# Which steps of two interleaved attentions wait for each other on TensorE

## The chip, the cores and the metric

One Trainium2 chip, one core. The metric is the device time of one execution in microseconds (us), as the median of a few executions. A kernel's profile is one more execution, with an instruction trace; its times are counted from the start of the span. TensorE is called PE, VectorE DVE, ScalarE ACT, GpSimd POOL, SyncE SP (it issues the loads).

## The reference

Two layers of an encoder on 272 tokens (16 meta tokens and a grid of 4 x 64) of width 2048, all in float32. In short:

```python
for l in range(2):
    gq, gk, gv, gr, glr, nq, nk, nv = split(h @ w_in[l])      # one projection, 6176 columns
    g = log_sigmoid(glr @ w_up + b_up) / 16                   # decay, forward and backward
    o = gla_scan(gq, gk, gv, g_fwd) + flip(gla_scan(flip(...), g_bwd))   # 4 heads, dk 128, dv 256
    y_gla = rms_norm(o) * norm_w * silu(gr)
    y_na = neighbourhood_attention(nq, nk, nv, rel_bias)      # 16 heads of 64, window 4 x 16 and the metas
    h = layer_norm(alpha * h + concat(y_gla, y_na) @ w_out)
    h = layer_norm(alpha * h + square(relu(h @ w_ff1)) @ w_ff2)   # 2048 -> 8192 -> 2048
```

The metas are dropped from the output (256 x 2048).

## The kernel before, in words

**Products.** Activations lie transposed, features on the partitions and tokens (272, or 256 where the metas are no longer needed) along the row. A float32 product is made of three single-pass products of a rounded type (fp32r): each operand is split into a high part (a rounding copy on ACT) and a low part (a subtraction on DVE), and high*high, low*high and high*low are added in PSUM. So every weight block of 128 x 1024 that SP loads is split on the way (`halves`, lines L217 on ACT and L218 on DVE; tiles `raw`, `wh`, `wl`, three buffers each). One output tile of 128 features is made in two halves: `eight` (L252) issues the products of one weight block, which are 24 at 272 columns, or 16 (at 512 and 256 columns in turn) where 256 tokens are enough, and two of them make an output. `by_k` (L293) and `sixteen` (L264) are the same work in other loops. These products are called main products below.

**What runs beside them.** While the projection's main products run, the two attentions are done piece by piece. Both are Python generators: each `yield` ends a step. `by_m` calls `pump(fg, bg, meet)` after every half output, and `pump` takes `fg` steps of the foreground queue and `bg` steps of the background queue; shares of a step are kept as credit. The linear attention's four heads (`gla_head`) are the background. While the gate columns r are projected it gets 1.3 steps a half (`GLA_R`), and while the 24 output tiles of the neighbourhood attention (q, k, v of eight pairs of heads) are projected it gets 1.4 (`GLA_NA`). The foreground has one step a half: the gates of the linear attention (`silu`), then the pairs of the neighbourhood attention (`na_pair`).

**Steps with products of their own.** Products whose operands were not split run as float32 in several passes: an instruction of this kind has two records in the trace.

- In `gla_head`: `group(0)` (L608 and L612, blocks of 32 columns), called G0 here; `group(4)` with L659, L663 and L667, called G4; then, after `am` and `parts` (the scores `A`, split by ACT at L319 and DVE at L320), the product of scores and values, L689 to L693, called o here, which is fp32r; then `mean` (split `sp`, product L934 with a matrix of 1/n), fp32r.
- In `na_pair`: the scores L747 and L751 of one pair, together with the output product L808 and L813 of the pair before (`na_out`), called N here; and the transposes L769 to L776, called T, which have one record each.

**Who waits.** A generator that yields True says that its next step should meet one of the other queue. `pump` holds such a step of the background back until a foreground step of the same kind ran in the same call, but at most `MEET` half outputs:

```python
            if self.bg and self.wants.get(self.bg[0]):
                alone = meet and not some
                if ran or alone and self.late < MEET:
                    self.late += alone and not ran
                    self.credit = min(self.credit, 2)
                    break
```

Even where nothing is met (`meet` is False while r is projected) the test `ran` makes such a step the first background step of its half.

**Order on the engines.** The program's order is not the order on an engine. A scheduler places each instruction by its priority and by when its own model of the chip says that the operands are there; on the chip each engine then runs its list in order, and waits where an operand is not there.

Of the kernel before, what the change touches and what calls it, by code (L numbers as in the profile page):

```python
# [31 lines left out]
EPS = 1e-5  # L32
TAU = 16.0
NEG = -1e30
GLA_R, GLA_NA, NORMS = 1.3, 1.4, (1.0, 0.6)
LEAD = 4
WARM = 14
MEET = 2
PAD = 40
PITCH = 288  # L40
WIDE = 1280
# [17 lines left out]
class Trunk:  # L59
# [66 lines left out]
    def pump(self, fg, bg, meet=False):  # L126
# [10 lines left out]
        while self.credit >= 1:  # L137
# [4 lines that stand above are left out]
# [417 lines left out]
    def gla_head(self, h):  # L559
# [117 lines left out]
        high, low = wide(parts, L), wide(parts[:, 1], L)  # L677
        self.split(wide(A, 3 * P), high, low)
        yield
        yield True  # L680
        while 2 * h + 1 not in self.gate:
            yield True
        os_ = []
        rs, tn = (g2.tile([P, L], F32, name=nm, tag=nm, bufs=1)[:, :n] for nm in ("grs", "gtn"))
        for e in range(2):
# [48 lines left out]
    def na_pair(self, c, q, k, v):  # L734
        nc, b = self.nc, self.a2
        heads = [slice(hh * NAD, hh * NAD + NAD) for hh in range(2)]
        two = lambda a: a.rearrange("p (t c) -> p t c", t=2)
        bias = b.tile([P, 4, NKEY], F32, name="nb", tag="nb")
        nc.sync.dma_start(bias, self.i["nab"][self.l, c])
        s = b.tile([P, 4, NKEY], F32, name="ns", tag="ns")  # L740
        st = b.tile([P, 12], F32, name="nst", tag="nst")
        if self.due:
            self.due()
        ps = self.spare(2)
        for t in range(2):
            for hh, hs in enumerate(heads):
                nc.tensor.matmul(ps[hh][:, t * NKEY:t * NKEY + NKEY], lhsT=q[hs, NM + t * P:NM + t * P + P], rhs=k[hs, t, :],  # L747
                                 start=True, stop=True)
        if self.full:
            for hh, hs in enumerate(heads):  # L750
                nc.tensor.matmul(ps[hh][:, 2 * NKEY:2 * NKEY + NK2], lhsT=q[hs, :P], rhs=k[hs, 0, P:],  # L751
                                 start=True, stop=True)
            meta = self.nms[c % 2]
            sm = meta[:NM, :, :NK2]
        for hh in range(2):
            nc.vector.tensor_tensor(s[:, 2 * hh:2 * hh + 2, :], two(ps[hh][:, :2 * NKEY]), bias[:, 2 * hh:2 * hh + 2, :], ALU.add)
            if self.full:
                nc.vector.tensor_tensor(sm[:, hh, :], ps[hh][:NM, 2 * NKEY:2 * NKEY + NK2], self.qmask, ALU.add)
        pr = self.npr[c % 2]
        self.softmax(s, st, 4, ((s[:, :, :P], s[:, :, :P]), (pr[:, :, :NK2], s[:, :, P:])))  # L760
        yield
        if self.full:
            mt = b.tile([NM, 6], F32, name="mst", tag="mst")
            self.softmax(sm, mt, 2, ((sm, sm),))
        yield
        yield True
        pv, *pts = self.bank(), *self.spare(2)
        for t in range(2):
            nc.tensor.transpose(pv[:, t * P:t * P + P], v[0][:, t, :], self.ident)  # L769
        nc.tensor.transpose(pv[:, T:T + P], v[1].rearrange("p t c -> p (t c)"), self.ident)  # L770
        for hh, pt in enumerate(pts):
            for t in range(2):
                nc.tensor.transpose(pt[:, t * P:t * P + P], s[:, 2 * hh + t, :P], self.ident)  # L773
            nc.tensor.transpose(pt[:, T:T + P], pr[:, 2 * hh:2 * hh + 2, :].rearrange("p u c -> p (u c)"), self.ident)
            if self.full and hh:
                nc.tensor.transpose(pt[:, T + P:], meta.rearrange("p u c -> p (u c)"), self.ident)  # L776
        v1 = b.tile([P, 2, P], F32, name="v1", tag="v1")
        v2 = b.tile([P, P], F32, name="v2", tag="v2")
        nc.scalar.copy(v1, two(pv[:, :T]))
        nc.vector.tensor_copy(v2, pv[:, T:T + P])  # L780
        p1 = b.tile([P, 4, P], F32, name="p1", tag="p1", bufs=1)
        p2 = b.tile([P, 2, P], F32, name="p2", tag="p2", bufs=1)
        for hh, pt in enumerate(pts):
            nc.scalar.copy(p1[:, 2 * hh:2 * hh + 2, :], two(pt[:, :T]))
            nc.vector.tensor_copy(p2[:, hh, :], pt[:, T:T + P])
        pm = None
        if self.full:
            pm = self.npm[c % 2]
            for hh, hs in enumerate(heads):
                nc.vector.tensor_copy(pm[hs, hh, :], pts[1][hs, T + P:T + P + NM])  # L790
        self.due = lambda: self.na_out(c, v1, v2, p1, p2, pm)
        yield True
        if c == 7:
            self.due()
            yield
# [131 lines left out]
    def mean(self, src, n, i=0, pool=None):  # L927

        parts = [t[:, :src.shape[-1]] for t in self.pair(pool or self.lp, "sp", i)]
        self.split(src, *parts)  # L930
        yield True
        p = self.bank()[:, :src.shape[-1]]
        for i, v in enumerate(parts):
            self.nc.tensor.matmul(p, lhsT=self.ones_r[n], rhs=v, start=i == 0, stop=i == 1)  # L934
        return p
# [297 lines left out]
```

## Time and profile before

| what | value |
|---|---|
| median of 3 executions | 2332.03 us (2331.26 to 2332.49) |
| the profiled execution, its span | 2332.43 us, 2330.6 us |
| PE busy | 2319.4 us, 100% of the span |
| DVE, ACT, POOL busy | 65%, 52%, 6% |
| granted PE clock | nine tenths or more in all 40 slices |
| DMA | 419.02 MB, 180 GB/s on average |

The stages that matter here: in layer 0 the columns of the neighbourhood attention are projected from 160 to 342 us, in layer 1 from 1346 to 1520 us, with r just ahead of them. A row of the timeline gives the start, the length, the engine, the source line and what is written and read; matmuls overlap one another, so the start of the next row tells more than the length. Four main products of 272 columns and the two after them are one group of six.

### The profile page before, as it was taken

To read this page: it belongs to the slowest core of one execution; us is meant where nothing else is said; L and a number is where in the kernel's file an instruction comes from. 1 tells how busy PE (TensorE), PEld (TensorE's weight loads), DVE (VectorE), ACT (ScalarE), POOL (GpSimd) and SP (SyncE) were. 2 spreads that over 40 slices of the span, in tenths; PEclk is the share of its full clock that TensorE was granted. 3 is DMA by queue.
4 is the path that set the end of the run, shared out by engine and by line. 5 is a ranking of instruction groups with operands and counts; after the bars stand their busy time and mean duration, and the time that the engine had idled before them with its cause. 6 is when DMAs were issued, how large, how long until landed. Compare 5 with 4: busy or idle time off the path is not lost.

```text
span 2330.6 us, 44637 instructions
## 1 busy us (share of the span) xinstructions
PE 2319.4 (100%) x18180; PEld 2208.1 (95%) x18180; DVE 1519.6 (65%) x2432; ACT 1221.6 (52%) x2100; POOL 129.4 (6%) x200
## 2 busy tenths in 40 slices
PE   9999999999999999999999999999999999999998
PEld 9999999999999999999999899989988888888888
DVE  5588777775544455547576887778866545666655
ACT  5666665564433344444456666655655334555443
POOL 0021110110000000000020111100100000000000
PEclk9999999999999999999999999999999999999999
DMA  8554445555555555555555555445665666666664
GB/s 264 155 163 153 153 142 173 175 178 181 180 181 181 180 180 177 180 181 180 179 180 170 175 161 164 158 155 190 190 196 189 194 197 188 193 197 214 199 194 149
DMA packets 118302, 419.02 MB, mean 180 GB/s; under 512 B 13513, under 2 KB 14025, under 8 KB 118097
## 3 DMA queue, kind: packets, MB, share of 16 engines
q1 hardware_dynamic: 117808, 415.65, 56.7%
q8 instruction: 142, 2.33, 0.4%
q14 instruction: 64, 0.52, 0.1%
q10 hardware_dynamic: 288, 0.52, 0.1%
HBM read 414.03 MB, written 2.10 MB: 179 GB/s over the span
## 4 chain that ended last, share of the span: by engine, by line
PE 97%; DVE 2%; ACT 1%; issue 0%; DMA 0%; SPq 0%; DVEq 0%; ACTq 0%
PE mm L252 57%; PE mm L264 29%; PE mm L293 6%; PE bg L293 1%; PE bg L808 1%; PE mm L747 1%; PE bg L608 1%; DVE wl L218 1%; PE bg L454 0%; ACT wh L217 0%; PE mm L773 0%; DVE acc L1036 0%; DMA raw<-in_win 0%; PE bg L934 0%; PE mm L497 0%
## 5 line engine op out<-in xcount | busy, mean ns | idle before, releaser
L218 DVE TENSOR_TENSOR wl<-raw,wh 128x1024 fp32r<-128x1024 f32 (+1 forms) x770 | 937.5, 1224 | 646.8 <-ACT wh L217 546.8
L217 ACT CAST wh<-raw 128x1024 fp32r<-128x1024 f32 (+1 forms) x770 | 805.7, 1047 | 794.0 <-PE mm L252 384.9
L252 PE MATMUL mm<-x,wh 128*128 128x272 f32 (+3 forms) x4544 | 805.7, 294 | 0.5 <-ACT ft L484 0.5
L252 PEld LDWEIGHTS mm<-x,wh 128*128 128x128 f32 x4544 | 646.7, 188 | 15.6 <-ACT ft L484 0.7
L252 PE MATMUL mm<-x,wl 128*128 128x272 f32 (+3 forms) x2432 | 519.6, 284 | 0.0
L252 PEld LDWEIGHTS mm<-x,wl 128*128 128x128 f32 x2432 | 390.8, 188 | 0.0
L252 PE MATMUL mm<-y,wh 128*128 128x272 f32 (+1 forms) x1440 | 235.0, 285 | 0.0
L252 PEld LDWEIGHTS mm<-y,wh 128*128 128x128 f32 x1440 | 199.7, 188 | 0.1
L264 PE MATMUL mm<-x,wh 128*128 128x512 f32 x832 | 193.8, 390 | 0.0
L264 PEld LDWEIGHTS mm<-x,wh 128*128 128x128 f32 x832 | 154.2, 188 | 31.0
L252 PE MATMUL mm<-u,wh 128*128 128x272 f32 (+1 forms) x1056 | 172.1, 285 | 0.0
L264 PE MATMUL mm<-y,wh 128*128 128x512 f32 x688 | 162.9, 390 | 2.0 <-ACT wh L217 2.0
L264 PEld LDWEIGHTS mm<-y,wh 128*128 128x128 f32 x688 | 128.6, 188 | 28.7 <-ACT wh L217 2.4
L252 PE MATMUL mm<-y,wl 128*128 128x272 f32 (+1 forms) x720 | 146.4, 284 | 0.0
L252 PEld LDWEIGHTS mm<-u,wh 128*128 128x128 f32 x1056 | 146.3, 188 | 0.0
L264 PE MATMUL mm<-u,wh 128*128 128x512 f32 x496 | 118.3, 390 | 0.0
L252 PEld LDWEIGHTS mm<-y,wl 128*128 128x128 f32 x720 | 112.6, 188 | 0.0
L264 PEld LDWEIGHTS mm<-u,wh 128*128 128x128 f32 x496 | 90.9, 188 | 17.7
L252 PE MATMUL mm<-u,wl 128*128 128x272 f32 (+1 forms) x528 | 107.3, 284 | 0.0
L264 PEld LDWEIGHTS mm<-x,wl 128*128 128x128 f32 x832 | 98.4, 188 | 2.0
L264 PE MATMUL mm<-x,wl 128*128 128x256 f32 x832 | 98.8, 276 | 0.0
L264 PEld LDWEIGHTS mm<-y,wl 128*128 128x128 f32 x688 | 84.2, 188 | 2.9
(277 smaller groups left out, 2325.8 us busy)
## 6 DMA issues: line engine op xcount, KB each, us to landing
raw<-in_wff SPq DMA_DIRECT2D x512, 512.0 KB, 3.6
raw<-in_win SPq DMA_DIRECT2D x190, 512.0 KB, 3.8
raw<-in_wout SPq DMA_DIRECT2D x64, 512.0 KB, 3.7
nb<-in_nab SPq DMA_DIRECT2D x16, 352.0 KB, 4.0
xraw<-in_xT SPq DMA_DIRECT2D x7, 272.0 KB, 4.6
out<-out SPq DMA_DIRECT2D x5, 256.0 KB, 3.1
brow<-in_norm SPq DMA_DIRECT2D x4, 256.0 KB, 5.5
gw<-in_wup SPq DMA_DIRECT2D x4, 196.0 KB
```

The lines of the kernel that those rows point to most:

```text
L217: self.nc.scalar.copy(h, r)
L218: self.wl = self.nc.vector.tensor_tensor(lo, r, h.bitcast(F32), ALU.subtract).ins
L252: mm(o, lhsT=self.block(w, j), rhs=rhs, start=first and not i, stop=last and i == len(TURNS[once]) - 1)
L264: self.nc.tensor.matmul(o, lhsT=self.block(both[j // 8][low], j % 8), rhs=rhs, start=first and not i + j, stop=bool(last and i and j == 15 ...
L293: self.nc.tensor.matmul(ps[g + m][:, :n], lhsT=self.block(parts[p][0], 4 * j + m if first else 2 * m + j), rhs=acts[k + j][parts[p][1]][:, ...
L608: nc.tensor.matmul(ps[b * 32:b * 32 + 32, o:o + w], lhsT=k[:, c:c + 32], rhs=q[:, r:r + w], start=True, stop=True)
L747: nc.tensor.matmul(ps[hh][:, t * NKEY:t * NKEY + NKEY], lhsT=q[hs, NM + t * P:NM + t * P + P], rhs=k[hs, t, :], start=True, stop=True)
L808: nc.tensor.matmul(po[t][hs, :P], lhsT=v2[ts, hs] if rest else v1[:, t, hs], rhs=p2[ts, hh, :] if rest else p1[:, 2 * hh + t, :], start=re ...
```

## The change

`MEET` goes from 2 to 5, `GLA_NA` from 1.4 to 1.8, and four `yield True` become plain `yield`: in `gla_head` ahead of o (and while the gates it needs are still missing), in `na_pair` ahead of the transposes T, and in `mean` ahead of its product. So o, T and the mean no longer wait for another queue's step nor for the first place in a half output; G0, G4 and N still do.

```diff
-GLA_R, GLA_NA, NORMS = 1.3, 1.4, (1.0, 0.6)
+GLA_R, GLA_NA, NORMS = 1.3, 1.8, (1.0, 0.6)
...
-MEET = 2
+MEET = 5
...
         self.split(wide(A, 3 * P), high, low)
         yield
-        yield True
+        yield
         while 2 * h + 1 not in self.gate:
-            yield True
+            yield
...
             self.softmax(sm, mt, 2, ((sm, sm),))
         yield
-        yield True
+        yield
         pv, *pts = self.bank(), *self.spare(2)
...
         self.split(src, *parts)
-        yield True
+        yield
         p = self.bank()[:, :src.shape[-1]]
```

What it does to PE's list, at three places. First, in layer 0, the G0 of the third head (its L608 and L612 read `qk_82`; `U` are its gathered operands). Before, it stands behind the transposes T of a pair:

```order
 L774 MATMUL mm<-ident,npr_2191 128x128
 L776 MATMUL mm<-ident,nms_2199 128x128
-L608 MATMUL bg<-qk_82 32x32 x8
-L612 MATMUL bg<-qk_82 32x16
-L608 MATMUL bg<-U,qk_82 32x32 x8
-L612 MATMUL bg<-U,qk_82 32x16
-L608 MATMUL bg<-U 32x32 x8
-L612 MATMUL bg<-U 32x16
-L608 MATMUL bg<-U 32x32 x8
-L612 MATMUL bg<-U 32x16
```

and now, 24 main products later, behind the scores of the same pair's successor (N):

```order
 L747 MATMUL mm<-nk,nq 128x176 x4
 L751 MATMUL mm<-nk,nq 128x48 x2
+L608 MATMUL bg<-qk_82 32x32 x8
+L612 MATMUL bg<-qk_82 32x16
+L608 MATMUL bg<-U,qk_82 32x32 x8
+L612 MATMUL bg<-U,qk_82 32x16
+L608 MATMUL bg<-U 32x32 x8
+L612 MATMUL bg<-U 32x16
+L608 MATMUL bg<-U 32x32 x8
+L612 MATMUL bg<-U 32x16
```

G0 has moved from T to N. The G4 of the third head moves in the same way, that of the second head from a place of its own to its first N, and layer 1 has the same three moves; the fourth head's G0 and G4 stood with an N before.

Second, o of the fourth head in layer 0, on PE (`x_552` and `x_555` are activations of main products, `wh` and `wl` weights). Its fourteen products stood in one row behind a T, 33 main products further on; now they start here:

```order
 L252 MATMUL mm<-x_487,wl 128x272
 L252 MATMUL mm<-x_552,wh 128x272 x2
-L252 MATMUL mm<-x_555,wh 128x272 x2
+L252 MATMUL mm<-x_555,wh 128x272
+L689 MATMUL bg<-parts,V 128x272 x2
+L252 MATMUL mm<-x_555,wh 128x272
 L252 MATMUL mm<-x_552,wl 128x272
 L252 MATMUL mm<-x_555,wl 128x272
+L690 MATMUL bg<-parts,V 128x272
+L691 MATMUL bg<-parts,y_92 128x272
```

The first two, L689, read the high part of `parts`; L690, three main products later, reads the low part. The G4 before them (behind the N that starts 39 main products earlier) has not moved. The second and the third head's o stand in the same way, 41 and 39 main products behind their N and G4; the products of `mean` (L934) follow singly. The first head's o stands, unbroken, 24 main products earlier than before (16 in layer 1).

Third, the same place in layer 1, on PE:

```order
 L252 MATMUL mm<-x_14330,wh 128x512
 L252 MATMUL mm<-x_14330,wl 128x256
+L689 MATMUL bg<-parts,V 128x256 x2
 L252 MATMUL mm<-x_14462,wh 128x512
 L252 MATMUL mm<-x_14462,wl 128x256
 L252 MATMUL mm<-x_14593,wh 128x512
+L690 MATMUL bg<-parts,V 128x256
+L691 MATMUL bg<-parts,y_14622 128x256
+L689 MATMUL bg<-parts,V 128x256
+L690 MATMUL bg<-parts,V 128x256
+L691 MATMUL bg<-parts,y_14622 128x256
+L693 MATMUL bg<-am,VS 128x256
```

Here o starts 28 main products behind its N and G4, as the third head's does; the second head's starts 43 behind. On ACT the list between G4 and the split `parts` is the same for the fourth head as before, and the third head's now reads the same.

## The prediction

> **What bounds the kernel now.** I read the page first: its busy times, and the shares of the chain that ended last.
>
> ```profile
> span 2330.6 us, 44637 instructions
> PE 2319.4 (100%) x18180; PEld 2208.1 (95%) x18180; DVE 1519.6 (65%) x2432; ACT 1221.6 (52%) x2100; POOL 129.4 (6%) x200
> PE 97%; DVE 2%; ACT 1%; issue 0%; DMA 0%; SPq 0%; DVEq 0%; ACTq 0%
> ```
>
> PE is hardly ever without work, and 97% of the chain is PE. So the change can act in two ways only: by how much of PE's time its own instructions take, and by how long PE stands before an operand. DVE (65% busy) and ACT (52%) are not full, but a chain of ten dependent pieces on them still takes microseconds; the timeline tells where PE meets such a chain.
>
> **Part one: fewer switches to float32.** The timeline of PE, around a G0 by itself, around an N, and around an N with a G0 behind it:
>
> ```profile
> 119.63 0.33 PE L608 MATMUL bg<-qk 128*32 128x32 f32 x16
> ...
> 120.49 0.77 PE L252 MATMUL mm<-x,wh 128*128 128x272 f32 x4
> ...
> 209.02 0.41 PE L252 MATMUL mm<-x,wl 128*128 128x272 f32 x2
> 209.36 1.04 PE L808 MATMUL bg<-p,v 64*64 64x128 f32 x16
> ...
> 211.35 0.76 PE L252 MATMUL mm<-x,wh 128*128 128x272 f32 x4
> 211.95 0.41 PE L252 MATMUL mm<-x,wl 128*128 128x272 f32 x2
> 212.19 0.65 PE L252 MATMUL mm<-x,wh 128*128 128x272 f32 x4
> ...
> 271.96 1.04 PE L808 MATMUL bg<-p,v 64*64 64x128 f32 x16
> ...
> 274.81 0.65 PE L252 MATMUL mm<-x,wh 128*128 128x272 f32 x3
> ```
>
> Two main products take 0.24 us from start to start (211.95 to 212.19), so one takes 0.12. Ahead of N two take 0.34 (209.02 to 209.36): entering costs 0.10. Behind N four take 0.60 (211.35 to 211.95) instead of 0.49: leaving costs 0.11. G0 is 0.86 us long, N 1.99, the two together 2.85. So the pair is entered and left once, and a meeting saves 0.2 us. With T it is different:
>
> ```profile
> 220.26 0.38 PE L769 MATMUL bg<-ident,nv 128*128 128x128 f32 x2
> ...
> 222.30 0.77 PE L252 MATMUL mm<-x,wh 128*128 128x272 f32 x4
> ...
> 283.75 0.38 PE L769 MATMUL bg<-ident,nv 128*128 128x128 f32 x2
> ...
> 284.76 0.73 PE L252 MATMUL mm<-x,wh 128*128 128x272 f32 x4
> ```
>
> T with a G0 behind it takes 2.04 us, T by itself 1.01 and G0 0.86: the 0.17 more is a switch between the two, so a G0 that meets T saves next to nothing.
>
> The lists show six steps that newly meet an N: in each layer the second head's G4, and the third head's G0 and G4. 6 x 0.2 = 1.2 us gained. Against it: in layer 0 the second head's L667 now stands a few main products behind its G4 and is entered and left by itself (0.2), and in layer 1 two T are broken up by a mean (from 0 to 0.4 each; I take 0.15). Net -0.7, between -1.2 and -0.2. That o and the mean meet nothing any more costs no switch: they are fp32r, as the main products are.
>
> The Trainium skill, TensorEngine Tiling (Array Packing), Key Properties, says that a change of the tiling mode drains TensorE, while a change of tile within a mode doesn't. By that rule N (blocks of 64) and G0 (blocks of 32 columns) would be different modes, a meeting would save nothing, and the sum below would come out 1.2 us higher. The trace disagrees: 1.99 and 0.86 us add up to just the 2.85 measured.
>
> **Part two: o comes ahead of its scores.** What a late operand costs is seen at the one place in these stretches where PE has one before, the mean of the first head in layer 1:
>
> ```profile
> 1333.93 0.28 PE L252 MATMUL mm<-x,wl 128*128 128x256 f32 x1
> 1334.81 0.39 PE L934 MATMUL bg<-sp,onesr 128*128 128x256 f32 x1 [0.61 <-ACT sp L319]
> 1335.04 0.40 PE L252 MATMUL mm<-x,wh 128*128 128x512 f32 x1
> ```
>
> At 0.12 us a product the L934 comes 0.76 late, and the product behind it follows after 0.23: a late operand costs its lateness and about 0.1 of refilling.
>
> Before, o waited for a T or an N, until well after `parts` was split. Now, by the credit of up to 2 + 1.8 steps, G4, `am` and the split fall into one half, and o into the next; only the scheduler's model holds it back, to the places shown in the lists. When `parts` is really there, ACT and DVE tell. The fourth head's N and G4 stand at the same places before and after, with the same list on ACT, so its times hold for after too. Layer 0 first, then layer 1:
>
> ```profile
> 297.77 0.37 ACT L664 COPY A<-bg 128x256 f32<-128x256 f32 x1 [1.36 <-PE bg L663]
> ...
> 302.88 0.65 ACT L319 CAST parts<-A 128x544 fp32r<-128x544 f32 x1
> 303.56 0.73 DVE L320 TENSOR_TENSOR parts<-A,parts 128x544 fp32r<-128x544 f32 x1 [0.68 <-ACT parts L319]
> ...
> 1483.36 0.62 ACT L319 CAST parts<-A 128x512 fp32r<-128x512 f32 x1
> ```
>
> and PE, where o will stand:
>
> ```profile
> 302.67 0.65 PE L252 MATMUL mm<-x,wh 128*128 128x272 f32 x4
> ...
> 1482.86 0.39 PE L252 MATMUL mm<-x,wh 128*128 128x512 f32 x1
> ```
>
> In layer 0 the high part ends at 302.88 + 0.65 = 303.53. The L689 of after stands behind three of the four main products that begin at 302.67, so PE reaches it at 302.67 + 3 x 0.12 = 303.03: 0.5 us early. In layer 1 the high part ends at 1483.98, and L689 takes the place of the product at 1482.86: 1.1 us early. Main products are queued behind it whose weights are ready; nothing overtakes a waiting matmul, so the loss reaches the end one to one.
>
> The third head has the same lists now, so again 0.5 and 1.1. The second head's o stands two main products later in layer 0 (0.5 - 0.25 = 0.25); in layer 1 it stands 43 behind its G4, where before shows nothing like it, and I take the 1.1 of the others, between 0.5 and 1.3. The sum is 1.25 + 3.3 = 4.55 us, and six refills are 0.6.
>
> **Part three: smaller waits.** The low part of `parts` ends on DVE at 304.29, 0.76 after the high part; L690 stands two L689 and three main products (0.6) behind, so it waits for 0.1 more in layer 0: 0.3 for three heads. The six products of the mean that now follow o without a meeting are like other single L934 of before; one of these:
>
> ```profile
> 1053.88 0.41 PE L252 MATMUL mm<-y,wl 128*128 128x272 f32 x2
> 1054.31 0.39 PE L934 MATMUL bg<-sp,onesr 128*128 128x272 f32 x1
> ```
>
> Two products ask for 0.24, and it comes after 0.43: 0.19 late. The worst is the 0.76 above, the best nothing. I take 0.15 for each of six, as in this row rather than the other: 0.9, from 0 to 3. In layer 1 the first head goes the other way: its mean now stands 32 main products behind o, so the 0.76 + 0.1 goes; but its o, 16 main products earlier, falls on this moment of PE, and of DVE:
>
> ```profile
> 1326.81 0.39 PE L252 MATMUL mm<-x,wh 128*128 128x512 f32 x1
> ```
>
> ```profile
> 1326.66 0.69 DVE L320 TENSOR_TENSOR parts<-A,parts 128x512 fp32r<-128x512 f32 x1 [2.19 <-ACT parts L319]
> ```
>
> The second product of o needs the low part, which ends at 1327.35, so 0.5 + 0.1 comes back: net -0.25. The longer patience (`MEET` 5) holds heads back, but in the lists the last o stands earlier than before, and nothing is left for the drain at the sixth group; SP's list differs in the place of one bias load. I put both at nothing. What covers them are the three weight buffers; without these, a block that comes late is one more wait of 0.76 + 0.1.
>
> **The sum.** -0.7 + 4.55 + 0.6 + 0.3 + 0.9 - 0.25 = +5.4 us on the profiled execution's 2332.43, so 2337.8. That execution lies 0.4 above the median of the runs, so the median becomes 2337.4, +0.23%.
>
> **Rivals.**
> - *A smaller loss.* Only the waits that before's own rows show come out in full: third and fourth head, 2 x (0.5 + 1.1) and four refills, 3.6; the second head half (0.7), the means nothing, switches -1.0, first head -0.25. That is +3, 2335. For it: ACT idles 1.36 us ahead of L664, so it is not behind. Against it: PE ends that idleness, so a chain can't begin before its G4.
> - *Faster.* The scheduler's places are right, o and the mean find their operands, and what stays is the 0.7 of switches and the 0.86 of the first head's mean: 2332.0 - 1.5 = 2330.5. It decides if `parts` comes 0.5 us sooner in layer 0 and 1.1 in layer 1. Against it: the list on ACT between G4 and `parts` is unchanged.
> - *Much slower.* The steps packed into one half push the weights' splits (L217, L218) behind them, and main products wait as well: one late block for each of six heads, 6 x 0.86 = 5.2 more, 2342.6. Against it: DVE is a third idle, and main products have no such wait in these stretches before.
> - *The change does not move what it says.* The lists exclude it.
>
> **How the numbers follow.** A measurement of this kernel can tell about 0.2% (4.7 us) from no change, so the border is at 2336.7. My forecast above that border has 0.53, the smaller loss (2332 to 2336.7) 0.37, faster 0.05 (over 0.2% of it 0.01), much slower 0.05. So slower 0.58, same 0.41, faster 0.01. The range goes down to +1.8, the smaller loss with the second head's wait gone and all of the 1.2 of switches, and up to +8.8, the sum with nearly all of the 3 for the means and the 1.3 for the second head: 2333.8 to 2340.8.
>
> **What would show it.** PE's waits in the profile after should name ACT's `parts` for L689, about 0.5 us in layer 0 and 1.1 in layer 1, two or three times each, and the wait of 0.6 for `sp` in the first head of layer 1 should be gone; N with G0 should still be 2.85 us. If PE does not wait for `parts`, part two is wrong and the time lies below 2332; if main products wait for `wl` or `wh` in these stretches, it is the third rival.

## The result, and the profile after

The changed kernel takes 2338.41 us (median of 7 runs, 2338.21 to 2339.82); the kernel before, measured again beside it, 2331.56 (7 runs, 2330.73 to 2332.49). The ratio is 1.0029, with a 95% interval from 1.0019 to 1.0038: slower by 0.29%, where 2337.4 and +0.23% were forecast. The profiled execution of after took 2338.21, with a span of 2336.4. Its page, and PE's waits (line, what it waited for, us in total, times, the longest):

```profile
span 2336.4 us, 44625 instructions
PE 2321.7 (99%) x18180; PEld 2209.5 (95%) x18180; DVE 1518.6 (65%) x2432; ACT 1221.4 (52%) x2100; POOL 140.1 (6%) x200
PE 94%; DVE 3%; ACT 2%; issue 1%; DMA 0%; POOL 0%; DVEq 0%; ACTq 0%; POOLq 0%
```

```profile
PE bg L689 <- ACT parts L319: 4.6, 6, 1.2
...
PE bg L690 <- DVE parts L320: 0.3, 1, 0.3
```

DVE's and ACT's busy times have not moved (1519.6 and 1221.6 before): the work is the same. New are these two waits: L689 waits six times for the high part of `parts`, which ACT makes, and L690 once for the low part from DVE. Gone is the wait of 0.6 us of the mean of the first head in layer 1. PE's share of the chain has gone from 97% to 94%, because at these waits the chain now runs back through the lists of ACT and DVE. Around the third head's o, in layer 0 and in layer 1, PE's timeline reads:

```profile
255.78 0.53 PE L252 MATMUL mm<-x,wh 128*128 128x272 f32 x3
256.69 0.52 PE L689 MATMUL bg<-parts,V 128*128 128x272 f32 x2 [0.39 <-ACT parts L319]
...
1440.37 0.28 PE L252 MATMUL mm<-x,wl 128*128 128x256 f32 x1
1441.67 0.50 PE L689 MATMUL bg<-parts,V 128*128 128x256 f32 x2 [1.03 <-ACT parts L319]
1442.01 0.39 PE L252 MATMUL mm<-x,wh 128*128 128x512 f32 x1
```

In layer 0 three products of 0.12 from 255.78 would bring L689 at 256.15; it comes at 256.69, 0.55 late (the 0.39 in brackets counts only from the modelled end of the matmul ahead). In layer 1 it should follow at 1440.49 and comes at 1441.67, 1.18 late; the main product behind it starts only after it, at 1442.01. ACT's timeline says why, from the end of G4's L663 to the end of `parts`; first the second head of layer 0, then the third, and at last one row of the second head of layer 1:

```profile
193.34 0.37 ACT L664 COPY A<-bg 128x256 f32<-128x256 f32 x1 [1.77 <-PE bg L663]
...
194.58 0.44 ACT L728 ACTIVATE ns<-ns,nst 128x176 f32<-128x176 f32 x1 [0.61 <-DVE nst L726]
...
199.06 0.64 ACT L319 CAST parts<-A 128x544 fp32r<-128x544 f32 x1
...
250.89 0.37 ACT L664 COPY A<-bg 128x256 f32<-128x256 f32 x1 [1.36 <-PE bg L663]
...
251.51 0.44 ACT L728 ACTIVATE ns<-ns,nst 128x176 f32<-128x176 f32 x1
...
253.23 0.19 ACT L628 COPY near<-bg 128x64 f32<-128x64 f32 x1
...
253.87 1.22 ACT L635 COPY A<-near 32x128 f32<-32x128 f32 x4
255.11 0.86 ACT L325 CAST am<-Am 16x272 fp32r<-16x272 f32 x2
256.00 0.65 ACT L319 CAST parts<-A 128x544 fp32r<-128x544 f32 x1
...
1380.97 0.64 ACT L638 COPY S<-qk 128x544 f32<-128x544 f32 x1
```

From 250.89 to 256.65 ACT works without a gap for 5.8 us, and a half output is only 3 us of PE. In front of the copies to `A` stand the exponentials of the softmax (L728) of the very N that G4 has met, 1.7 us (251.51 to 253.23); behind them four small copies (L635, 1.2) and the two casts to `am` (0.86), and only then `parts`. In the second head of layer 0 ACT also waits 0.61 us for DVE between G4 and the exponentials; in that of layer 1 a copy for the next head (L638, 0.64 us) stands there.

### The profile page after: what moved, and what is told of

Its sections match the earlier page's. It is cut to its first block, busy times and chain, and to the rows that moved or that the text cites. A ratio compares the mean times of both kernels' runs of the same rounds, so it can differ in the third digit from the quotient of the medians.

```text
span 2336.4 us, 44625 instructions
## 1 busy us (share of the span) xinstructions
PE 2321.7 (99%) x18180; PEld 2209.5 (95%) x18180; DVE 1518.6 (65%) x2432; ACT 1221.4 (52%) x2100; POOL 140.1 (6%) x200
## 4 chain that ended last, share of the span: by engine, by line
PE 94%; DVE 3%; ACT 2%; issue 1%; DMA 0%; POOL 0%; DVEq 0%; ACTq 0%; POOLq 0%
PE mm L252 55%; PE mm L264 29%; PE mm L293 6%; PE bg L293 1%; DVE wl L218 1%; PE bg L808 1%; ACT ns L728 0%; PE mm L747 0%; ACT wh L217 0%; PE bg L454 0%; PE bg L608 0%; ACT A L635 0%; PE bg L934 0%; PE mm L773 0%; DVE acc L1036 0%
```

## The experiments

Each was measured beside the kernel before on the same chip; ratios are to that. The expectations are counted from 2331.6 or 2332.3 us for the kernel before, which measured 2332.34 beside `only_o_unmet`, `only_numbers`, `one_half_later` and `credit_2`, 2332.70 beside `o_and_mean_from_stored` and 2332.03 beside the others; so it is the distances to it that are to be compared. Edits are to the changed kernel unless another is named.

**Two parts of the change, each by itself.** `only_o_unmet` is the kernel before (1.4 steps, MEET 2) with only o's two `yield True` made plain; `only_numbers` is the kernel before with the two numbers alone.

```diff
@@ only_o_unmet, from the kernel before
-        yield True
+        yield
         while 2 * h + 1 not in self.gate:
-            yield True
+            yield
@@ only_numbers, from the kernel before
-GLA_R, GLA_NA, NORMS = 1.3, 1.4, (1.0, 0.6)
+GLA_R, GLA_NA, NORMS = 1.3, 1.8, (1.0, 0.6)
-MEET = 2
+MEET = 5
```

> Before with one edit of the change, o's yield True made plain: at 1.4 steps a half o stands at the start of a half output 45 or more main products behind its G4. Theory: no wait for parts; G0 and G4 still meet what they met, so 2331.6 - 0.3 = 2331.3 us. Rival (taking the meeting from o costs by itself, whatever the rate): most of the 6.8 us, 2337.

> Before with MEET 5 and 1.8 steps a half, all yield True kept. Theory: o still meets a T or an N and so finds its scores; two steps newly meet an N, less one L667 by itself: 2331.6 - 0.2 = 2331.4 us. Rival (patience and packing cost the time): 2336 to 2338.

Measured: 2332.30 for the first (ratio 1.0001, 0.9992 to 1.0010) and 2333.45 for the second (1.0008, 0.9999 to 1.0017), before 2332.34. Neither by itself loses what the whole change loses. In the first, the o of the second to fourth heads stands 48 main products behind its G4, where the changed kernel has 28 to 43; and G4 stands by itself or behind a T, so that no exponentials of an N (1.7 us) lie ahead of `parts` on ACT. PE waits for `parts` once only, for 0.3 us, in the first head of layer 1. How much is due to the place and how much to the shorter list was not separated. In the second, these o still meet a T or an N, 64 or 72 main products behind G4. It lies 1.1 us above the kernel before, where 0.2 below was expected: PE waits there at two places that were not in the expectation,

```profile
PE bg L667 <- DVE Am L626: 0.6, 1, 0.6
...
PE bg L659 <- DVE S L594: 0.3, 1, 0.3
```

both inside G4: L659 comes before DVE has merged `S`, L667 before it has copied into `Am`. With their refills they are some 1.3 us, which is the difference.

**Only o meets again.** The changed kernel with o's two `yield True` back; the mean and T stay plain.

```diff
-        yield
+        yield True
         while 2 * h + 1 not in self.gate:
-            yield
+            yield True
```

> The changed kernel with o's two `yield True` put back; 1.8 steps, MEET 5 and the plain yields ahead of T and of the mean stay. o stands behind an N again, at least 72 main products after its G4, but the fourth head comes so late that its G4 and o are drained at the sixth group, 26 products apart. Theory: no wait for `parts` in the first three heads; in the fourth some 0.55 and 1.2 with refills, and two G4 entered by themselves (0.4), so 1.8 over before: 2334.1. Rival (T and mean, or the numbers alone, carry the loss): 2337 or more.

Measured: 2335.51 (1.0013, 1.0004 to 1.0022). The waits for `parts` are gone in three heads and stay in the fourth, which is pushed to the end; PE's waits are

```profile
PE bg L689 <- ACT parts L319: 1.2, 2, 0.8
PE bg L934 <- ACT sp L319: 0.9, 1, 0.9
```

and the two L689 lie 0.57 and 0.96 late, as the theory had it (0.55 and 1.2). The second line, the mean of layer 1's first head, stood in before too. The run lies 3.5 us above the kernel before, where 1.8 was expected, so the sum was 1.7 too low: the six means now split from o come up to 0.22 late, 0.56 together, the second head's L667 comes 0.28 late as in the changed kernel, and the rest, some 0.8, is not assigned. So with T, the mean and the numbers left as in the change, o's plain yield carries about half of the loss of 6.85; of what stays, most is the same wait at the fourth head and its G4 by itself, and the means have a small part.

**o one half output later, and the credit alone.** Both have one more `yield` ahead of o. With 1.9 steps o comes one half later; with 2.0 the added step is paid for, and the o of the second to fourth heads stands just where the changed kernel has it.

```diff
@@ one_half_later
-GLA_R, GLA_NA, NORMS = 1.3, 1.8, (1.0, 0.6)
+GLA_R, GLA_NA, NORMS = 1.3, 1.9, (1.0, 0.6)
...
-        yield
+        yield; yield
         while 2 * h + 1 not in self.gate:
@@ credit_2: the same with 2.0 for 1.9
```

> The changed kernel with one more yield ahead of o and 1.9 background steps a half instead of 1.8: G0, G4 and N meet as in the changed kernel, but every o stands unbroken at the next half output, 6 to 9 main products later. Theory (o stands ahead of its scores): no L689 waits for parts, the switches saved (about 1.0 us, as no T is broken up) and the first head's mean (0.86) stay, so 2331.6 - 1.8 = 2329.8 us. Rival (the longer patience and the steps packed into one half cost the time, by DVE and ACT): about 2338, as the changed kernel.

> The same kernel as one_half_later but with 2.0 steps a half: the added yield is taken up by the credit, and o stands just where the changed kernel has it for the second to fourth heads (41, 39, 39 main products behind in layer 0, 43, 28, 28 in layer 1). Theory: L689 waits as in the changed kernel, 5.5 us in all; only the first head of layer 1 is spared its 0.6, so 2337.8 us. Rival (the yield itself, or steps spread over more halves, help): as one_half_later, about 2330.

Measured: `one_half_later` 2335.23 (1.0015, 1.0006 to 1.0023) and `credit_2` 2339.12 (1.0033, 1.0020 to 1.0045). The second came out as the theory said: another step and other numbers, the same place of o, the same wait (4.7 us, six times) and the same loss (6.8 us above the kernel before, against 6.85). The first did not: 2.9 us of the loss stay, where a gain of 1.8 was expected. The expectation had o 6 to 9 main products later and took that to be enough for every L689. In the second to fourth heads o came 4 to 9 main products later, which is 0.7 to 1.1 us, and in layer 1 it had been 1.18 to 1.36 late. PE's waits in the second and the third head of layer 1 show what was left:

```profile
1384.77 0.38 PE L689 MATMUL bg<-parts,V 128*128 128x256 f32 x1 [0.63 <-ACT parts L319]
1385.49 0.38 PE L690 MATMUL bg<-parts,V 128*128 128x256 f32 x1 [0.34 <-DVE parts L320]
...
1439.38 0.38 PE L689 MATMUL bg<-parts,V 128*128 128x256 f32 x1 [0.32 <-ACT parts L319]
1440.11 0.39 PE L690 MATMUL bg<-parts,V 128*128 128x256 f32 x1 [0.34 <-DVE parts L320]
```

And because o is no longer split up, L690 follows L689 at once and now waits for the low part as well: DVE's subtraction starts when ACT's cast is done and takes 0.69 us.

**A shorter list on ACT.** `one_half_later`, with the split of `parts` ahead of the stacking of `am`; PE's list does not change.

```diff
-        am = g2.tile([80, L], F32R, name="am", tag="am", bufs=1)[:, :n]
-        nc.gpsimd.memset(am.bitcast(F32), 0.0)
-        self.stack(Am[:, :n], am, NM, (0, 64), 32)
-        yield
         wide = lambda t, w: bass.AP(t.tensor, t.offset, [t.ap[0], [w, 2], [1, n]])
         parts = g2.tile([P, 4, 2, L], F32R, name="parts", tag="U", bufs=1)
         high, low = wide(parts, L), wide(parts[:, 1], L)
         self.split(wide(A, 3 * P), high, low)
+        yield
+        am = g2.tile([80, L], F32R, name="am", tag="am", bufs=1)[:, :n]
+        nc.gpsimd.memset(am.bitcast(F32), 0.0)
+        self.stack(Am[:, :n], am, NM, (0, 64), 32)
         yield; yield
```

> one_half_later with the split of `parts` ahead of the stacking of `am` in the program, so that one of the two ACT casts of 0.42 us (L325) leaves the chain between G4 and `parts`; PE's list is the same as that of one_half_later. Theory (the remaining wait is the length of ACT's list between G4 and `parts`): each o that was late by 0.4 or more gains 0.42, the others what they were late, 2.2 in all: 2335.2 - 2.2 = 2333.0. Rival (the wait begins with G4 on PE, or with the low part on DVE, whatever ACT's order): 2335.2.

Measured: 2333.28 (1.0005, 0.9997 to 1.0014), as the theory had it to 0.3 us. Counted from the kernel before, the 2.9 us of `one_half_later` have become 1.25; the intervals of the two runs overlap, so it is the trace that shows what went. In layer 1, ACT and then PE:

```profile
1437.16 0.41 ACT L325 CAST am<-Am 16x256 fp32r<-16x256 f32 x1
1437.47 0.61 ACT L319 CAST parts<-A 128x512 fp32r<-128x512 f32 x1
1438.11 0.40 ACT L325 CAST am<-Am 16x256 fp32r<-16x256 f32 x1
```

```profile
1438.08 0.28 PE L252 MATMUL mm<-x,wl 128*128 128x256 f32 x1
1438.19 0.33 PE L689 MATMUL bg<-parts,V 128*128 128x256 f32 x1
1438.87 0.38 PE L690 MATMUL bg<-parts,V 128*128 128x256 f32 x1 [0.34 <-DVE parts L320]
```

One cast of 0.4 us behind `parts` instead of ahead of it, and the wait for the high part of this head is gone. So it is the length of ACT's list behind G4 that sets the wait for the high part; the wait for DVE's low part stays. This is the best order found in which G4 meets an N and o meets nothing; it does not beat the kernel before.

**The waits taken away.** In `o_from_stored`, o reads tiles that have been ready for long; in `o_and_mean_from_stored` the linear attention's mean does so too (the constants of `ones_r`, repeated along the row). Neither computes the attention any more: what o makes of its scores is left out.

```diff
@@ o_from_stored
-                nc.tensor.matmul(o, lhsT=v, rhs=high[:, i, :], start=not i, stop=False)
-                nc.tensor.matmul(o, lhsT=v, rhs=low[:, i, :], start=False, stop=False)
-                nc.tensor.matmul(o, lhsT=vl, rhs=high[:, i, :], start=False, stop=False)
+                nc.tensor.matmul(o, lhsT=v, rhs=self.vlow[h][:, :n], start=not i, stop=False)
+                nc.tensor.matmul(o, lhsT=v, rhs=self.vlow[h][:, :n], start=False, stop=False)
+                nc.tensor.matmul(o, lhsT=vl, rhs=self.vlow[h][:, :n], start=False, stop=False)
...
-            nc.tensor.matmul(o, lhsT=self.VS[:, c], rhs=am, start=False, stop=True)
+            nc.tensor.matmul(o, lhsT=self.VS[:, c], rhs=self.VS[:, :n], start=False, stop=True)
```

> This is the changed kernel, but o (L689 to L693) reads `vlow` and `VS`, which lie ready since long, in place of `parts` and `am`: the number of products, their shapes and types are the same, the result is not, and the splits are still done. o can't wait any more. Theory (the loss is o's wait for `parts`): the lateness seen in the changed kernel goes, 0.68 + 0.56 + 0.55 in layer 0 and 1.36 + 1.18 + 1.18 in layer 1, with six refills of 0.1 and the 0.7 of the first head of layer 1: 2338.4 - 6.8 = 2331.6. Rival (the loss is in the packing itself: steps that stand closer cost PE, ACT or DVE time wherever o finds its operands): 2337 or more.

> o_from_stored, with the product of the linear attention's mean (L934) reading the stored constants of `ones_r` in place of `sp`: now neither o nor the mean can wait, and the result is that of neither. The products, the splits and all of ACT's and DVE's work stay. Theory (o_from_stored only handed o's wait on to the mean, because ACT's list behind G4 is what is late): the lateness of the six means, 0.83 + 0.03 + 0.69 + 0.03 + 0.38 + 0.36 in layer 0 and 1.19 + 1.25 + 0.95 in layer 1, goes as well: 2337.1 - 5.7 = 2331.4. Rival (something else in the packing costs the 5 us, and PE's wait only shows where): the loss comes back at another step, 2336 or more.

Measured: `o_from_stored` 2337.09 (1.0021, 1.0012 to 1.0029), 5.1 above the kernel before, where the theory had it level. The scheduler put o at the head of its half, where nothing held it, and the wait came back one step later:

```profile
PE bg L934 <- ACT sp L319: 4.3, 6, 1.1
```

Six waits again, 4.3 us, but for the mean's `sp`. The squares of o (L694) and the split of `sp` are ACT's work, and on ACT they stand behind the same list, here in the third head of layer 1:

```profile
1440.62 0.62 ACT L319 CAST parts<-A 128x512 fp32r<-128x512 f32 x1
1441.26 0.38 ACT L694 ACTIVATE grs<-bg 128x256 f32<-128x256 f32 x1
1441.55 0.38 ACT L694 ACTIVATE gtn<-bg 128x256 f32<-128x256 f32 x1
1441.81 1.05 ACT L217 CAST wh<-raw 128x1024 fp32r<-128x1024 f32 x1
...
1443.29 0.41 ACT L319 CAST sp<-grs 128x256 fp32r<-128x256 f32 x1
```

So the expectation that the wait belongs to o alone was wrong; here it passed to the next product that needs ACT. `o_and_mean_from_stored` takes both away: 2333.81 (1.0006, 0.9996 to 1.0015), 1.1 above the kernel before, and PE waits for neither; within the noise the loss is gone. The median is 2.4 above the expectation, of which 0.7 is that the kernel before was slower here than beside `o_from_stored`. The profiled execution, 2332.38, is the quickest of the runs, and holds one wait that no other profile has, 1.8 us:

```profile
PE mm L747 <- POOL nk L523: 1.8, 1, 1.8
```

That is a score of N, for a copy of keys on POOL (the last section). Without it this execution would be at 2330.6, by an estimate from these two numbers. The runs go up to 2335.24, and what varies between them was not found out.

**Later still.** Four more `yield` ahead of o, with 2.0 steps.

```diff
-GLA_R, GLA_NA, NORMS = 1.3, 1.8, (1.0, 0.6)
+GLA_R, GLA_NA, NORMS = 1.3, 2.0, (1.0, 0.6)
...
-        yield
+        yield; yield; yield; yield; yield
         while 2 * h + 1 not in self.gate:
```

> The changed kernel with four more `yield` ahead of o and 2.0 steps a half: o of the second and third head follows the T that comes 72 (in layer 1: 64) main products after G4, that of the first head stands 144 behind, and nothing is split up; the fourth head's G4 comes by itself and its o 26 products behind it. Theory: only the fourth head's o waits, 0.55 + 1.2 with two refills; G4 by itself 0.4; gains of 0.7 for the other meetings and 0.9 for the first head's mean: 2332.3 + 0.4 = 2332.7. Rival (o's place is not what matters, the numbers are): 2335 or more.

Measured: 2334.93 (1.0012, 1.0003 to 1.0021), 2.9 above the kernel before, where 0.4 was expected. Where o is late enough it waits no longer (second and third head), and in the fourth it waits as foreseen; but

```profile
PE bg L689 <- ACT parts L319: 1.1, 2, 0.7
PE bg L934 <- DVE sp L320: 0.8, 1, 0.8
PE bg L667 <- DVE Am L626: 0.7, 1, 0.7
...
PE bg L934 <- ACT sp L319: 0.3, 1, 0.3
```

L667 and the mean wait at three other places, 1.8 us, which with their refills is 2.1 of the missing 2.5.

## Why the prediction was right

The mechanism was the one forecast, and it was shown by the runs that move or remove it: o stands ahead of its scores, PE waits for ACT's `parts`, and what is queued behind starts later by as much. The size came out in part by luck, since two errors of opposite sign offset each other. Point by point:

- **Part two, the wait of o.** The third and the fourth head came as read from before's ACT rows: 0.5 predicted and 0.55 measured in layer 0, 1.1 and 1.18 in layer 1. Mis-sized were the second heads, 0.25 and 1.1 predicted, 0.68 and 1.36 measured. The prediction had ACT's list run as in the other heads and only moved o; but in layer 0 ACT stands there 0.61 us before the exponentials, for DVE (194.58 above), and in layer 1 a copy of 0.64 for the next head stands in front of them (1380.97 above); from the end of G4 to the end of `parts` it takes 0.6 us longer than in the third head, in both layers. All lateness: 5.5 us, against 4.55. With the refills, and with o's products split up in two pieces, the six o's cost 6.4, against 5.15.
- **Part three.** The low part costs nothing where o is split up: L690 is within 0.03 us of its place. Predicted was 0.3. The six means lose 0.5, against 0.9: in layer 0 the first of the two products is 0.05, 0.14 and 0.13 late, in layer 1 none waits. The first head of layer 1 is net 0.16 shorter, against 0.25. Its mean's wait is gone, and o waits instead, for the low part, as predicted:

```profile
1328.55 0.38 PE L689 MATMUL bg<-parts,V 128*128 128x256 f32 x1
1329.28 0.39 PE L690 MATMUL bg<-parts,V 128*128 128x256 f32 x1 [0.34 <-DVE parts L320]
```

- **Part one, the switches.** N with G0 is unchanged:

```profile
273.37 1.04 PE L808 MATMUL bg<-p,v 64*64 64x128 f32 x16
...
275.36 0.33 PE L608 MATMUL bg<-qk 128*32 128x32 f32 x16
...
276.22 0.77 PE L252 MATMUL mm<-x,wh 128*128 128x272 f32 x4
```

  2.85 us from N's first product to the first main product behind G0, as before. What is left of the difference of the two traces, when the waits above are taken off, is -0.7 (6.0 for all of PE's side products, less 6.4, plus 0.16, less 0.5). That this is the -0.7 predicted shows little. The o's of before, too, lost about 0.1 each behind their T or N, and counted against these the six cost 5.8 more, which leaves -0.2, the upper end of the forecast; three T, not two, are broken up by a mean in layer 1, and cost 0.5 more with their means than before, not 0.15. This was read from the traces of the two kernels; no run measures it by itself.

  The prediction's sentence that the trace disagrees with the tiling rule goes too far. From N's first product to what follows it takes 1.99 us, be it a main product (209.36 to 211.35) or G0 (273.37 to 275.36). Both are changes of the blocks, so a cost that both have can't be seen in these rows; and as N and G0 by themselves make four such changes and together three, a meeting would save one by that rule too. The rows show the 0.2 that a meeting saves, and not which mechanism it comes from.
- **MEET 5, the drain and SP's order** cost nothing that shows: no main product of these stretches waits, and `only_numbers`, which has MEET 5, loses 1.1 us, for which two waits inside G4 account. `credit_2` has the changed kernel's time with another credit.
- **The sum** was +5.4 on the profiled execution, which came out 5.8 longer; PE's side products grew by 6.0: 1.25 more for o, 0.6 less for part three. Between the medians it is 6.85, since the profiled execution of before lay 0.9 above the median of the runs now measured, and that of after 0.2 below.
- **The ends of the range** do not follow from the terms named for them: these add up to +2.2 and +7.7, not +1.8 and +8.8. The measured +6.85 lies inside either.

Of the rivals, *a smaller loss* had doubted the second heads, and these turned out the largest. *Much slower* needed main products to wait for `wh` or `wl`: none does in these stretches. *Faster* would have needed `parts` sooner; `split_first_later` shows how far that goes, and that it takes another place of o as well.

## What to carry to other kernels

Steps that are lifted from a meeting come as soon as the schedule lets them, and PE then stands before the longest list of the engine that feeds it: read the dependent engine's list between the two steps (here 5.8 us on ACT, against 3 us of PE in a half output) before letting them fall into neighbouring slots. A wait removed at one product can return at the next one fed by the same engine, unless that list gets shorter: taking away o's operands altogether gained 1.8 us of 6.85, and reordering one cast of 0.4 us on ACT, in `split_first_later`, gained 1.6 (both as distances to the kernel before, each uncertain by about 2 us). And a step that costs by being held back may be paying for exactly the time that its operand needs.

## What the runs showed of the hardware

The wait of L747 in `o_and_mean_from_stored` comes from copies of keys on POOL (L523), of 128x32 elements, which took 0.42 us in the median and 6.1 us once. First the copy just ahead of that one, in POOL's timeline, and the line's group (shortest, median and longest in ns); then DVE in that stretch:

```profile
1491.57 1.82 POOL L523 COPY nk<-nk 128x32 f32<-128x32 f32 x1 [16.91 <-ACT nk L519]
...
L523 POOL COPY nk<-nk x32: 203/420/6113, 173.3 to 1514.9; 128x32 f32<-128x32 f32 x32
```

```profile
1492.10 1.22 DVE L218 TENSOR_TENSOR wl<-raw,wh 128x1024 fp32r<-128x1024 f32 x1
1493.24 0.18 DVE L520 COPY nk<-mm 128x32 f32<-128x32 f32 x1
1493.34 2.09 DVE L403 TENSOR_TENSOR acc<-x 128x256 f32<-128x256 f32 x6
1495.35 1.22 DVE L218 TENSOR_TENSOR wl<-raw,wh 128x1024 fp32r<-128x1024 f32 x1
1496.48 1.76 DVE L403 TENSOR_TENSOR acc<-x 128x256 f32<-128x256 f32 x5
1498.16 1.22 DVE L218 TENSOR_TENSOR wl<-raw,wh 128x1024 fp32r<-128x1024 f32 x1
1499.30 0.18 DVE L520 COPY nr<-mm 128x32 f32<-128x32 f32 x1
```

The first copy ends at 1493.39. The second, the one of 6.11, begins at 1493.34 in the trace and ends at 1499.45. Each end is 0.15 us behind the start of a DVE copy from PSUM (L520), and between these two, DVE has subtractions and sums of two operands end to end. By its record the copy lasted as long as this row of DVE did. The Trainium skill, SBUF — State Buffer, Who interferes with whom, says that a VectorE instruction with two SBUF inputs contends with a GpSimd instruction that reads SBUF, and calls the port pair that they share an exclusive lock. The rows agree, to 0.15 us at both ends, in one execution; no run here was made to test it. If that is the cause, it is a price of packing DVE without gaps that none of the theories had.
